# Hybrid FNet and SSD encoder layer: the SSD products of a unit moved to every second slot of the projection

## Chip, cores and metric

The kernel runs on one core of one Trainium2 chip. The metric is the device time of a whole execution in microseconds (us), given as the median of several runs. Five engines work side by side, each through its own queue in order: TensorE (PE, matrix products; its weight loads are listed as PEld), VectorE (DVE), ScalarE (ACT), GpSimd (POOL) and SyncE (SP), which issues nearly all DMA transfers. They wait for one another by semaphores.

## What is computed

Two sequences, of 1024 and 2048 tokens of 1024 features, pass through one encoder layer in float32. Cut to what matters here:

```python
u = rms_norm(h, norm_w)
proj = u @ w_in
z_f, u_f, z_s, xbc, dt_raw = split(proj)
xs, Bm, Cm = split(silu(conv5(xbc)))
# SSD per head, in chunks of 128 tokens, forwards and backwards:
cb     = einsum('bclgn,bcsgn->bclsg', Cc, Bc)
y_diag = einsum('bclsg,bclsgr,bcsgrp->bclgrp', cb, decay, X)
states = einsum('bcsgn,bcsgr,bcsgrp->bcgrpn', Bc, decay_st, X)
y_off  = einsum('bclgn,bcgrpn,bclgr->bclgrp', Cc, prev, exp(a_cs))
y_s = (y_fwd + y_bwd + D * xs) * silu(z_s)     # then a norm by groups
y_f = fnet(u_f) * silu(z_f)
h = h + concat([y_f, y_s]) @ w_out
h = h + (p @ w_ple_in) * sigmoid(h @ w_ple_gate)
out = rms_norm(h, final_norm_w)
```

## The kernel before

**Three stages follow one another.** The first, some 1880 us long, is the projection with the SSD; the second is the Fourier mixing; the third holds the output products. The change touches the first.

The tokens are worked in three blocks of 1024: `P` (the short sequence), `S1` and `S2` (the halves of the long one). A block's projection is cut into **jobs** of 128 output columns, and a job into three **pieces** of 342 tokens. A piece is 24 matmuls into one of three PSUM tiles `ps` (line 361): each float32 product is made of three, high by high, high by low and low by high. The weights of a job come in one DMA (`wr`, line 182); ACT rounds them to the high part `wh` (line 189) and POOL subtracts to get the low part `wl` (line 190).

The 24 heads are worked in twelve **units** of two. A unit's column job `x` is convolved and put through SiLU (DVE and ACT), and its SSD parts then follow, each with a few small float32 matmuls into one of five PSUM banks (the pool `bg`, taken in turn):

- `tokens` (line 421): four transposes into `ptt`; ACT copies them to `xm`.
- `weighted` (line 586): POOL makes `xw` from `xm` and the decay weights. The two buffers of `xw` are shared by the four calls of a unit, `(d, c4)` for direction and half.
- `states` (line 606): products of `xw` and `Bm` into `pst`; DVE runs the state on in `H` (line 617).
- `diag` (line 574): products with the decay tile `R`, into `pd`. `R` is loaded by SP (`rows_in`, three buffers), cut by POOL (line 549), exponentiated by ACT (line 558) and joined by DVE (lines 563 and 565).
- `across` (line 648): products of `H` and `CT` into `po`; DVE adds them to `y` (lines 651 and 652).
- `gated` (line 657): POOL multiplies `y` by the gate. In block `S1` alone it does two more operations, on `er` and `zT` (lines 661 and 662).
- `group_tokens` and `group_cb` do the like once for three units (lines 421 and 525).

**The order is written out by hand.** Time is counted in **slots**, one for each piece. `pre(s, f)` puts a function ahead of the piece of slot s, `post(s, f)` behind it, and `step` runs the functions ahead, the piece, and the functions behind, in the order in which they were registered. Each engine's queue keeps that order. A unit's plan begins at slot s0, and consecutive units of a block are nine slots apart: s0 is 12 + 9u in `P`, 135 + 9u in `S1`, 258 + 9u in `S2`, so even and odd s0 take turns. The weight splits (`wh`, `wl`) were registered first of all; in the steady part they stand ahead of every third slot, at s0, s0 + 3, s0 + 6, s0 + 9 and so on. At a block's end the transposes `pt` of the next block's tokens (line 264) stand behind pieces too and take the same five banks.

So ahead of slot s0 + 9 stands, in POOL's queue: the split of a job's weights, `gated(4)` of the unit before (whose offset is 18 there), then what `weighted` has in this slot.

Of the kernel before, what the change touches and what calls it, by code (L numbers as in the profile page):

```python
# [56 lines left out]
def tile_hybrid_encoder(ctx: ExitStack, tc: tile.TileContext, a):  # L57
# [44 lines left out]
    with ExitStack() as ph:  # L102
# [175 lines left out]
        def pre(s_, fn, *args):  # L278
            assert s_ >= slot[0], (s_, slot[0])
            before.setdefault(s_, []).append((fn, args))  # L280

        def post(s_, fn, *args):
            assert s_ >= slot[0], (s_, slot[0])
            behind_.setdefault(s_, []).append((fn, args))
# [244 lines left out]
        class Unit:  # L529
# [140 lines left out]
            def plan(self, s0):  # L670

                B, g = self.B, self.g
                self.y, self.xw, self.er, self.H, self.R, self.xm = {}, {}, {}, {}, {}, {}
                if self.u % 3 == 0:
                    for k, s_ in enumerate((1, 3) if g else (4, 5)):
                        post(s0 + s_, group_tokens, B, g, 4 * k)
                    for k, s_ in enumerate((6, 7)):
                        post(s0 + s_, group_cb, B, g, 4 * k)
                post(s0 + 7, self.tokens, 0)
                pre(s0 + 8, self.weighted, 0, 0)  # L680
                post(s0 + 8, self.tokens, 4)
                pre(s0 + 6, self.state_in)
                pre(s0 + 9, self.weighted, 1, 4)
                post(s0 + 9, self.states, 0, 0)
                pre(s0 + 10, self.weighted, 0, 4)
                post(s0 + 10, self.states, 1, 4)
                pre(s0 + 11, self.weighted, 1, 0)
                post(s0 + 11, self.states, 0, 4)
                post(s0 + 12, self.states, 1, 0)
                pre(s0 + 11, self.decays, 0)  # L690
                pre(s0 + 13, self.decays, 4)
                for p in range(4):
                    s_ = s0 + 4 + 2 * p
                    pre(s_, self.rows_in, p)
                    pre(s_ + 2, self.rows_cut, p)
                    pre(s_ + 3, self.rows_exp, p)
                    pre(s_ + 4, self.rows_joined, p)
                    post(s_ + 5, self.diag, p)
                post(s0 + 14, self.across, 0)
                pre(s0 + 16, self.gated, 0)  # L700
                pre(s0 + 18, self.out, 0)
                post(s0 + 16, self.across, 4)
                pre(s0 + 18, self.gated, 4)
                pre(s0 + 20, self.out, 4)

        def norm_piece(b, i):

# [44 lines left out]
        for m in range(2, len(coming)):  # L752
            j, k = coming[m], coming[m - 1]
# [19 lines left out]
        with tc.manual_schedule():  # L773
# [30 lines left out]
            for B, js, what in rows_:  # L804
                bi, s0 = B.bi, slot[0]
                if what == "first":
                    q = s0 if bi else s0 + 1
# [459 lines left out]
    fn = q4.tile([P, DM], F32, name="fn")  # L1267
# [116 lines left out]
```

## Time and profile before

| | |
|---|---|
| Median of 3 runs | 2940.09 us (2939.32 to 2940.15) |
| The profiled execution | 2938.98 us, of which the span from first to last instruction is 2937.0 us |
| Mean granted TensorE clock | 0.983 of full speed |
| PE busy | 2806.8 us (96%) |
| DVE, ACT, POOL busy | 2223.1, 1382.3, 1515.5 us (76, 47, 52%) |

In a timeline a row gives the start, the length, the engine, the line, the operation, its output and inputs, the shapes and the number of merged instructions; in brackets stands how long the engine sat idle before it, and what released it. Matmuls overlap, so the distance from one start to the next tells what a matmul costs, not its own length. A float32 product of the SSD shows as two matmul records. In a table of waits a row gives the sum of the waits, their number and the longest. In a table by windows the columns are the length, the busy time of each engine with its number of instructions, the granted PE clock, the share of the DMA engines and GB/s.

### The profile page before, as it was taken

To read this page: it belongs to the slowest core of one execution; us is meant where nothing else is said; L and a number is where in the kernel's file an instruction comes from. 1 tells how busy PE (TensorE), PEld (TensorE's weight loads), DVE (VectorE), ACT (ScalarE), POOL (GpSimd) and SP (SyncE) were. 2 spreads that over 40 slices of the span, in tenths; PEclk is the share of its full clock that TensorE was granted. 3 is DMA by queue.
4 is the path that set the end of the run, shared out by engine and by line. 5 is a ranking of instruction groups with operands and counts; after the bars stand their busy time and mean duration, and the time that the engine had idled before them with its cause. 6 is when DMAs were issued, how large, how long until landed. Compare 5 with 4: busy or idle time off the path is not lost. (4 is left out here: it accounts for less than half of the span.)

```text
span 2937.0 us, 46503 instructions
## 1 busy us (share of the span) xinstructions
PE 2806.8 (96%) x17252; PEld 2551.2 (87%) x17252; DVE 2223.1 (76%) x3412; ACT 1382.3 (47%) x2980; POOL 1515.5 (52%) x1114
## 2 busy tenths in 40 slices
PE   6999999999999999999999999789999899989998
PEld 5999999999999999999999999777777677768887
DVE  3787777687778686778787776797989998766665
ACT  4544465444545564435444444344334533355554
POOL 1255656542667777633656655455877678510000
PEclk9999999999999999999999999889999999999999
DMA  3245565362465665534455454465544654442221
GB/s 99 85 146 153 167 188 168 126 182 83 125 186 165 207 190 157 160 118 116 145 161 157 154 159 132 151 230 213 173 154 145 230 167 140 150 180 80 95 97 62
DMA packets 327998, 440.10 MB, mean 150 GB/s; under 512 B 19824, under 2 KB 250932, under 8 KB 323932
## 3 DMA queue, kind: packets, MB, share of 16 engines
q1 hardware_dynamic: 327484, 436.08, 47.1%
q8 instruction: 136, 2.23, 0.3%
q10 hardware_dynamic: 288, 1.05, 0.1%
q14 instruction: 90, 0.74, 0.1%
HBM read 328.41 MB, written 109.71 MB: 149 GB/s over the span
## 5 line engine op out<-in xcount | busy, mean ns | idle before, releaser
L361 PE MATMUL ps<-uh,wh 128*128 128x342 f32 (+1 forms) x2880 | 955.3, 332 | 12.9 <-ACT uh L267 9.6
L361 PE MATMUL ps<-ul,wh 128*128 128x342 f32 (+1 forms) x2880 | 920.0, 319 | 2.5 <-DVE ul L268 2.5
L361 PE MATMUL ps<-uh,wl 128*128 128x342 f32 (+1 forms) x2880 | 921.7, 320 | 0.4 <-POOL wl L190 0.4
L190 POOL TENSOR_TENSOR wl<-wr,wh 128x1024 fp32r<-128x1024 f32 x120 | 296.3, 2469 | 660.4 <-ACT wh L189 660.4
L361 PEld LDWEIGHTS ps<-uh,wh 128*128 128x128 f32 x2880 | 545.2, 189 | 36.5 <-issue 15.5
L361 PEld LDWEIGHTS ps<-ul,wh 128*128 128x128 f32 x2880 | 548.2, 190 | 4.2 <-DVE ul L268 3.5
L361 PEld LDWEIGHTS ps<-uh,wl 128*128 128x128 f32 x2880 | 544.6, 189 | 1.2 <-POOL wl L190 1.1
L558 ACT ACTIVATE R<-R,lb 128x128 f32<-128x128 f32 x1152 | 352.9, 393 | 16.9 <-POOL R L549 16.8
L549 POOL TENSOR_SCALAR_AFFINE_SELECT R<-R 128x512 f32<-128x512 f32 x288 | 274.3, 974 | 6.8 <-DMA R<-ROWd 6.8
L617 DVE SCALAR_TENSOR_TENSOR H<-H,cd,pst 128x64 f32<-128x64 f32 x888 | 182.7, 276 | 102.7 <-PE pst L606 100.5
L586 POOL TENSOR_TENSOR xw<-xm,wd 128x512 f32<-128x512 f32 x144 | 189.4, 1326 | 137.2 <-ACT xm L423 111.7
L367 ACT COPY raw<-ps 128x342 f32<-128x342 f32 x180 | 78.9, 439 | 339.3 <-PE ps L361 339.2
L1100 PE MATMUL X<-whP,ah 128*128 128x512 f32 x480 | 196.8, 410 | 7.9 <-ACT pu L1109 4.7
L402 DVE SCALAR_TENSOR_TENSOR xT<-raw,cvt,xT 128x1024 f32<-128x1024 f32 x144 | 195.5, 1358 | 2.6
L1100 PE MATMUL X<-whP,al 128*128 128x512 f32 x480 | 193.7, 403 | 1.6 <-DVE al L1071 1.6
L1100 PE MATMUL X<-wlP,ah 128*128 128x512 f32 x480 | 194.2, 405 | 0.1
L1212 POOL TENSOR_TENSOR ht<-ht,pu 128x512 f32<-128x512 f32 x96 | 156.3, 1637 | 63.0 <-ACT pu L1109 44.0
L652 DVE TENSOR_TENSOR y<-y,yt 128x512 f32<-128x512 f32 (+1 forms) x144 | 161.3, 1120 | 5.0
L1071 DVE TENSOR_TENSOR al<-s,ah 128x512 fp32r<-128x512 f32 x144 | 142.9, 1014 | 20.2 <-ACT ah L1070 20.0
L272 ACT ACTIVATE zT<-ps 128x342 f32<-128x342 f32 (+1 forms) x108 | 49.1, 454 | 219.0 <-PE ps L361 218.7
L565 DVE TENSOR_TENSOR R<-R,cb 128x512 f32<-128x512 f32 x144 | 148.4, 1030 | 5.0
L651 DVE TENSOR_TENSOR yt<-po,er 128x512 f32<-128x512 f32 (+1 forms) x144 | 91.2, 634 | 76.0 <-PE po L648 67.8
(264 smaller groups left out, 5812.9 us busy)
## 6 DMA issues: line engine op xcount, KB each, us to landing
R<-ROWd SPq DMA_DIRECT2D x144, 512.0 KB
wr<-in_w_in SPq DMA_DIRECT2D x120, 512.0 KB
er<-EXPd SPq DMA_DIRECT2D x144, 256.0 KB
Hd<-ht SPq DMA_DIRECT2D x48, 512.0 KB
ht<-Hd SPq DMA_DIRECT2D x48, 512.0 KB
y<-Yd SPq DMA_DIRECT2D x46, 512.0 KB
wlP<-WSd SPq DMA_DIRECT2D x21, 1024.0 KB
Yd<-y SPq DMA_DIRECT2D x72, 256.0 KB
```

The source lines that it names most:

```text
L190: G.tensor_tensor(wl, raw, wh.bitcast(F32), op=ALU.subtract)
L361: T.matmul(ps[:, :n], lhsT=wt[:, kt, :], rhs=ut[:, kt, :n], start=(i == 0), stop=(i == 3 * KT - 1))
L402: V.scalar_tensor_tensor(dst, raw[:, k:k + TB], cvt[:, 20 * k + ct:20 * k + ct + 1], dst, op0=ALU.mult, op1=ALU.add)
L549: G.affine_select(out=R, in_=R, pattern=[[0, 2], [0, 2], [sgn, P]], compare_op=ALU.is_ge, fill=NEG, base=0, channel_multiplier=-sgn)
L558: S.activation(R[:, h, d, c, :], R[:, h, d, c, :], AF.Exp, bias=self.B.lb[:, 2 * p + c, hc + h:hc + h + 1])
L565: V.tensor_tensor(E[0], E[0], cb.unsqueeze(1).broadcast_to([P, 2, 2 * P]), op=ALU.mult)
L586: G.tensor_tensor(xw, self.xm[c4].rearrange("p c (h e) -> p c h e", h=2), col(self.B.wd[:, c4:c4 + 4, hc:hc + 2]).broadcast_to([P, 4, 2, 6 ...
L617: V.scalar_tensor_tensor(dst[:, e], H[d][:, cc, e], B.cd[:, cc, hc + h:hc + h + 1], pst[:, c, e], op0=ALU.mult, op1=ALU.add)
L652: V.tensor_tensor(y[:, cr], y[:, cr], t[:, cr], op=ALU.add)
L1071: V.tensor_tensor(al, src, ah.bitcast(F32), op=ALU.subtract)
L1100: T.matmul(ps, lhsT=at[:, k, :], rhs=wt[:, k, :], start=(first and i == 0), stop=(i == 11), skip_group_check=not first)
L1212: return lambda t: G.tensor_tensor(h, h, t, op=ALU.add)
```

## The change

The SSD parts of a unit are put only behind pieces of even slots: a new helper `part` rounds the slot up to the next even one, and `weighted` stands ahead of the slot behind the part that it needs.

```diff
+                def part(o, fn, *args):
+                    o += (s0 + o) % 2
+                    post(s0 + o, fn, *args)
+                    return s0 + o
                 if self.u % 3 == 0:
-                    for k, s_ in enumerate((1, 3) if g else (4, 5)):
-                        post(s0 + s_, group_tokens, B, g, 4 * k)
-                    for k, s_ in enumerate((6, 7)):
-                        post(s0 + s_, group_cb, B, g, 4 * k)
-                post(s0 + 7, self.tokens, 0)
-                pre(s0 + 8, self.weighted, 0, 0)
-                post(s0 + 8, self.tokens, 4)
+                    for k, o in enumerate((1, 3) if g else (4, 5)):
+                        part(o, group_tokens, B, g, 4 * k)
+                    for k, o in enumerate((6, 7)):
+                        part(o, group_cb, B, g, 4 * k)
                 pre(s0 + 6, self.state_in)
-                pre(s0 + 9, self.weighted, 1, 4)
-                post(s0 + 9, self.states, 0, 0)
-                pre(s0 + 10, self.weighted, 0, 4)
-                post(s0 + 10, self.states, 1, 4)
-                pre(s0 + 11, self.weighted, 1, 0)
-                post(s0 + 11, self.states, 0, 4)
-                post(s0 + 12, self.states, 1, 0)
+                pre(part(7, self.tokens, 0) + 1, self.weighted, 0, 0)
+                pre(part(8, self.tokens, 4) + 1, self.weighted, 1, 4)
+                pre(part(9, self.states, 0, 0) + 1, self.weighted, 0, 4)
+                pre(part(10, self.states, 1, 4) + 1, self.weighted, 1, 0)
+                part(11, self.states, 0, 4)
+                part(12, self.states, 1, 0)
...
-                    post(s_ + 5, self.diag, p)
-                post(s0 + 14, self.across, 0)
-                pre(s0 + 16, self.gated, 0)
-                pre(s0 + 18, self.out, 0)
-                post(s0 + 16, self.across, 4)
-                pre(s0 + 18, self.gated, 4)
-                pre(s0 + 20, self.out, 4)
+                    part(9 + 2 * p, self.diag, p)
+                for o, c4 in ((14, 0), (16, 4)):
+                    q = part(o, self.across, c4)
+                    pre(s0 + o + 2, self.gated, c4)
+                    pre(s0 + o + 4, self.out, c4)
```

Where s0 is even, both `tokens` stand at s0 + 8, both `weighted` of the first pair ahead of s0 + 9, the first two `states` with `diag(0)` at s0 + 10, the other two `weighted` ahead of s0 + 11, and the other two `states` at s0 + 12; each `diag` stands one slot later. Where s0 is odd, `tokens(4)` joins `states(0, 0)` at s0 + 9, the middle two `states` stand at s0 + 11, the last at s0 + 13, and `across` at s0 + 15 and s0 + 17. Loads, cuts, exponentials, joins and gates keep their slots. PE's projection is interrupted by SSD groups 346 times before and 190 times now; the matmuls are the same.

On PE, the place is unit 3 of block `S1` (s0 = 162): its second `tokens` (`ptt_9269`), the first two `states` (`pst`) and `diag(0)` (`pd_9340`). The rows `ps` are the first or last matmul of a piece. Before:

```order
L421 MATMUL ptt_9269<-ident_105,xT_8926 128x128 x4
L361 MATMUL ps_9300<-uh0_6616,wh_9102 128x342
...
L606 MATMUL pst_9328<-xw_9226,Bm_8878 128x128 x4
L574 MATMUL pd_9340<-R_9016,xm_9219 64x128 x4
L361 MATMUL ps_9361<-uh1_6774,wh_9102 128x342
...
L606 MATMUL pst_9388<-xw_9284,Bm_8878 128x128 x4
```

The same place of the changed kernel (`ptt_9267` is the second `tokens`, `pst_9368` and `pst_9381` the two `states`):

```order
L421 MATMUL ptt_9267<-ident_105,xT_8904 128x128 x4
L361 MATMUL ps_9300<-uh0_6609,wh_9087 128x342
...
L361 MATMUL ps_9300<-uh0_6609,wl_9088 128x342
L361 MATMUL ps_9340<-uh1_6761,wh_9087 128x342
...
L606 MATMUL pst_9368<-xw_9282,Bm_8937 128x128 x4
L606 MATMUL pst_9381<-xw_9284,Bm_8937 128x128 x4
L574 MATMUL pd_9393<-R_9000,xm_9259 64x128 x4
```

Two pieces now follow each other with nothing between, and both `states` stand behind the second.

In POOL's queue the same unit's `weighted` calls (`xw`), a weight split (`wl`) and the gates of the unit before (`y`, `er`, `zT`) stand in this order before:

```order
L657 TENSOR_TENSOR y_8944<-y_8944,zT_8456 128x512
L661 TENSOR_TENSOR er_8889<-er_8889,elt_154 128x512
L662 TENSOR_TENSOR zT_8456<-er_8889,zT_8456 128x512
L586 TENSOR_TENSOR xw_9226<-xm_9219,wd_7447 128x512
L549 AFFINE_SELECT R_9112<-R_9112 128x2x256 x2
L190 TENSOR_TENSOR wl_9276<-wr_9159,wh_9275 128x1024
L657 TENSOR_TENSOR y_9150<-y_9150,zT_8456 128x512
L661 TENSOR_TENSOR er_9005<-er_9005,elt_154 128x512
L662 TENSOR_TENSOR zT_8456<-er_9005,zT_8456 128x512
L586 TENSOR_TENSOR xw_9284<-xm_9268,wd_7447 128x512
L586 TENSOR_TENSOR xw_9347<-xm_9268,wd_7447 128x512
```

and now:

```order
L549 AFFINE_SELECT R_9097<-R_9097 128x2x256 x2
L190 TENSOR_TENSOR wl_9274<-wr_9159,wh_9273 128x1024
L657 TENSOR_TENSOR y_9135<-y_9135,zT_8437 128x512
L661 TENSOR_TENSOR er_8989<-er_8989,elt_154 128x512
L662 TENSOR_TENSOR zT_8437<-er_8989,zT_8437 128x512
L586 TENSOR_TENSOR xw_9282<-xm_9259,wd_7447 128x512
L586 TENSOR_TENSOR xw_9284<-xm_9266,wd_7447 128x512
L549 AFFINE_SELECT R_9206<-R_9206 128x2x256 x2
L586 TENSOR_TENSOR xw_9400<-xm_9266,wd_7447 128x512
```

The first `xw` of the unit, which stood ahead of the weight split and the gate, now stands behind them.

## The prediction

> **What bounds the kernel now.** First the page's totals, then the table by windows, then PE's waits in the first stage.
>
> ```profile
> span 2937.0 us, 46503 instructions
> PE 2806.8 (96%) x17252; PEld 2551.2 (87%) x17252; DVE 2223.1 (76%) x3412; ACT 1382.3 (47%) x2980; POOL 1515.5 (52%) x1114
> ...
> 300.00:400.00 100.00, 100.00 (x712) 97.27 (x712) 73.97 (x128) 52.80 (x124) 61.66 (x48) 1.00 0.62 189
> 900.00:1000.00 100.00, 99.38 (x704) 95.74 (x703) 78.72 (x135) 50.57 (x117) 66.89 (x53) 1.00 0.60 190
> ...
> PE prw L495 <- ACT acs L473: 4.6, 3, 2.6
> PE pst L606 <- POOL xw L586: 3.4, 9, 0.9
> PE pt L264 <- DVE H L617: 2.6, 2, 2.0
> ```
>
> In the first stage PE is never free: 100.00 us busy of 100, at full clock. The waits come from the window from 100 to 1880 us, and they are the longest three there; PE waits for little more than 10 us in 1780. So what the change is worth is (a) what an interruption of the projection costs on PE itself, and (b) the waits that it removes or makes. POOL and DVE are off the path as long as they hand over in time; (b) asks whether they still do.
>
> **What an interruption costs.** Three places on PE: `diag` alone between pieces, `across` alone (its last four matmuls shown again, from a narrower window), and `diag` with a further group behind it.
>
> ```profile
> 901.76 0.31 PE L361 MATMUL ps<-uh,wl 128*128 128x342 f32 x1
> 902.00 0.66 PE L574 MATMUL pd<-R,xm 128*64 128x128 f32 x8
> 902.59 0.42 PE L361 MATMUL ps<-uh,wh 128*128 128x342 f32 x1
> 902.85 0.31 PE L361 MATMUL ps<-ul,wh 128*128 128x342 f32 x1
> ...
> 906.33 0.32 PE L361 MATMUL ps<-uh,wl 128*128 128x342 f32 x1
> 906.48 1.72 PE L648 MATMUL po<-CT,H 128*128 128x128 f32 x14
> 907.60 0.61 PE L648 MATMUL po<-CT,H 128*128 128x128 f32 x4
> 907.96 0.40 PE L361 MATMUL ps<-uh,wh 128*128 128x342 f32 x1
> 908.20 0.31 PE L361 MATMUL ps<-ul,wh 128*128 128x342 f32 x1
> ...
> 252.77 0.32 PE L361 MATMUL ps<-uh,wh 128*128 128x342 f32 x1
> 252.92 0.32 PE L361 MATMUL ps<-ul,wh 128*128 128x342 f32 x1
> 253.08 0.31 PE L361 MATMUL ps<-uh,wl 128*128 128x342 f32 x1
> 253.32 0.66 PE L574 MATMUL pd<-R,xm 128*64 128x128 f32 x8
> 253.91 1.16 PE L525 MATMUL pc<-CT,BT 128*128 128x128 f32 x8
> 254.82 0.40 PE L361 MATMUL ps<-uh,wh 128*128 128x342 f32 x1
> 255.06 0.32 PE L361 MATMUL ps<-ul,wh 128*128 128x342 f32 x1
> ```
>
> Undisturbed, projection matmuls start 0.157 us apart (252.77 to 253.08 is two steps). The first one behind a group looks dear: the next starts 0.24 us later (907.96 to 908.20), 0.084 more. But it also starts early, close behind the group's last matmul. Whole: from 906.33 to 908.20 are 1.87 us; less two steps of 0.157 the 14 `po` matmuls cost 1.56, 0.111 each, and that is their pace inside the group (906.48 to 907.60 is ten steps, 0.112 each). Going in and out is free. `diag` alone costs 902.85 - 901.76 - 0.31 = 0.78. `diag` with eight `pc` behind it costs 255.06 - 253.08 - 0.31 = 1.67, and apart the two would be 0.78 + 8 x 0.111 = 1.67. **So joining two groups saves nothing:** 156 interruptions fewer are 0 us, and with 0.02 us of reading error each -3 to +3.
>
> **What the change removes.** All nine waits of `pst` for `xw` (3.4 us) are of the old order. In the new one an odd s0 gives POOL longer: below, POOL has its second `xw` 11.7 us after slot s0 + 9 begins, and PE asks for it only after three pieces (3 x 3.77) and that slot's group (4 `ptt`, 8 `pst`, 8 `pd`: 0.44 + 0.89 + 0.67), at 13.3. That is -3.4 us. Even s0 comes next.
>
> **What it adds: POOL in block S1.** The rows are of unit 3, whose slot s0 + 9 begins at 877.52, and of unit 7, which begins at 1059.97.
>
> ```profile
> 877.52 0.40 PE L361 MATMUL ps<-uh,wh 128*128 128x342 f32 x1
> 879.42 2.39 POOL L190 TENSOR_TENSOR wl<-wr,wh 128x1024 fp32r<-128x1024 f32 x1 [2.20 <-ACT wh L189]
> 881.76 1.28 POOL L657 TENSOR_TENSOR y<-y,zT 128x512 f32<-128x512 f32 x1
> 883.00 1.05 POOL L661 TENSOR_TENSOR er<-er,elt 128x512 f32<-128x512 f32 x1
> 884.13 1.65 POOL L662 TENSOR_TENSOR zT<-er,zT 128x512 f32<-128x512 f32 x1
> 885.74 3.48 POOL L586 TENSOR_TENSOR xw<-xm,wd 128x512 f32<-128x512 f32 x2
> 887.29 1.16 PE L606 MATMUL pst<-xw,Bm 128*128 128x128 f32 x8 [0.31 <-POOL xw L586]
> ...
> 1059.97 0.40 PE L361 MATMUL ps<-uh,wh 128*128 128x342 f32 x1
> 1067.84 2.51 POOL L586 TENSOR_TENSOR xw<-xm,wd 128x512 f32<-128x512 f32 x2
> ```
>
> Before, the `xw` ahead of the split was for the first `states`, and these two were for the later ones. Now the chain split, `y`, `er`, `zT` stays, since it hangs on ACT's `wh` and on the slot, and **both** `xw` that PE needs next stand behind it, while PE gets there sooner, for slot s0 + 9 has nothing behind its piece. PE asks after two pieces: 48 x 0.157 + 0.084 = 7.62 us. In unit 3 the first `xw` is ready at 887.29 - 877.52 = 9.77: a wait of 2.1. The eight `pst` then take 0.9, to 10.7, and the second is ready at 885.74 + 3.48 = 889.22, that is 11.7: another 1.0. In unit 7 the pair is shorter: the first, at half of 2.51, ends at 9.13 (1.5 late), the second at 10.38 (0.3 late). Blocked behind the waiting `pst` is all of PE, projection and all, so each microsecond counts in full. Even s0 in S1 means six units; the last has no split in that slot, which leaves five. Ends: 5 x 3.1 = 16, and 5 x 1.3 = 6.5 if POOL also starts 0.2 earlier and only the first wait stays. I take 2.3 each, since a first wait as in unit 3 with a second as in unit 7 is 2.4: **+11.5 us**.
>
> In `P` and `S2` the gate is one operation, and the same place has room:
>
> ```profile
> 400.70 0.40 PE L361 MATMUL ps<-uh,wh 128*128 128x342 f32 x1
> 406.18 2.55 POOL L586 TENSOR_TENSOR xw<-xm,wd 128x512 f32<-128x512 f32 x2
> ```
>
> The pair ends at 408.73, 8.03 us in; the first, near 6.8, is early, and the second is asked for at 7.62 + 0.9 = 8.5. Cost 0, with 0.5 us to spare.
>
> **The clock.** A gap on PE can cost more than itself:
>
> ```profile
> 729.77 0.42 PE L361 MATMUL ps<-uh,wh 128*128 128x342 f32 x1 [2.32 <-DVE zT L273]
> ...
> 729.77:733.60 3.83, 3.83 (x14) 3.83 (x15) 3.03 (x4) 1.27 (x2) 1.57 (x2) 0.56 0.99 303
> 733.60:737.00 3.40, 3.40 (x27) 3.40 (x27) 1.42 (x3) 3.40 (x12) 0.00 (x0) 1.00 0.25 97
> ```
>
> After this gap of 2.32 us the granted clock was 0.56 for 3.83 us, and 14 matmuls took what 24 take: 1.6 us lost. The nine old `xw` waits, 0.9 at most, left no such mark in windows at 1.00. My gaps of 1.5 to 2.1, in unit 3 with another of 1.0 close behind, lie between. I let three of five lose 1.5: **+4.5 us**, ends 0 and 8. The Trainium skill, "TensorE: Matmul & The Clock Gate", part 1, says that the clock falls to half after at least one idle window of about 3.4 us. By that rule none of these gaps would cost more than itself and the sum would be 4.5 lower; the row of 2.32 us speaks against it.
>
> **The rest.** At the two block ends the transposes `pt` wait for banks that DVE's `H` empties (2.6 us before). New there: two `pst` are emptied one behind the other, but PE has `pd` and two `pt` in between; 0, ends -2 and +4. Behind the very last piece one more `states` stands, whose run of `H` is 1.24 us by the row below: +1, ends 0 and 2.
>
> ```profile
> 1868.46 1.24 DVE L617 SCALAR_TENSOR_TENSOR H<-H,cd,pst 128x64 f32<-128x64 f32 x6
> POOL R L549 <- DMA R<-ROWd: 6.8, 3, 3.5
> ```
>
> Where s0 is even, the load of the fourth `R` needs the buffer of the first, whose `diag` is a slot later; SP holds its queue as long. POOL cuts that `R` two slots later and waited for such loads only 6.8 us in the first stage: hidden. DVE gets its evictions in bunches but the same sum; `ps` has three tiles, and the joined `R` of an even s0 now has a slot more. The later stages hold the same instructions, some in another order at the start of the Fourier stage and of the last products: 0, ends -3 and +3.
>
> **Sum**, against the profiled execution (2938.98: span 2937.0 and 1.98 around it; 1.1 below the median 2940.09): 0 - 3.4 + 11.5 + 4.5 + 0 + 1 + 0 = +13.6, so **2952.6 us**. All lower ends give 2934, all upper ends 2971.
>
> **Rivals.**
> 1. *The clock holds* (the rule above): 13.6 - 4.5 = +9.1, 2948.1. For it: no gap before of this very length. Chance 0.20.
> 2. *POOL's chain shortens*, as DVE is quieter beside it and ACT's split comes earlier: 6.5 - 3.4 + 1 = +4.1, 2943.1. For it: unit 7's pair takes 2.51 where unit 3's takes 3.48. Chance 0.20.
> 3. *Faster: an interruption does cost 0.084*, the late second start, and the early first start is no return for it. 156 x 0.084 = 13.1; with rival 2's waits -9.0, 2930.0. It decides if a slot without a group is shorter than 24 x 0.157. Against it: the 1.56 us of 14 `po`. Chance 0.07.
> 4. *DVE's bunches reach PE*: `R` or `H` comes late in every unit. At half a run of `H`, 0.6, that is 36 x 0.6 = 21.6 more, 2974. Against it: DVE's share, 76%. Chance 0.09.
>
> **Chances.** The forecast with its clock losses has 0.42, and 0.02 are left for the unforeseen. Slower by over 0.2% (5.9 us, about what a measurement here can tell from no change) are the forecast, rivals 1 and 4: 0.73 with the rest. Within 0.2%: rival 2, 0.20. Faster: 0.07. The range runs from 2940, below rival 2, to 2966, over the forecast with most of its upper ends; rivals 3 and 4 stay out.
>
> **What would show it.** Right: PE waits for `pst` on `xw` rise from 3.4 to about 11 us, all in S1, two to a unit of odd number, none in `P` and `S2`; the clock falls behind some; two joined pieces and a group still make 48 x 0.157 plus the group. Wrong: no such wait (POOL ahead), a shorter slot (rival 3), or waits on `H` or `R` throughout (rival 4).

## The result and the profile after

| | before | changed |
|---|---|---|
| Median, four runs each | 2939.70 us (2939.22 to 2940.15) | 2965.91 us (2957.86 to 2967.18) |
| Ratio of the runs (that of the medians alone is 1.0089) | | 1.0085, interval 1.0073 to 1.0097 |
| The profiled execution | 2938.98 us (span 2937.0) | 2957.86 us (span 2956.1), the shortest of its four |

The changed kernel is 26.2 us slower in the median and 18.9 us slower in the profiled execution. Two lines of its page, and then PE's waits of the first stage (100 to 1900 us), in the view that the prediction began with:

```profile
span 2956.1 us, 46441 instructions
PE 2816.4 (95%) x17252; PEld 2559.4 (87%) x17252; DVE 2220.9 (75%) x3412; ACT 1384.5 (47%) x2980; POOL 1524.9 (52%) x1114
...
PE pst L606 <- POOL xw L586: 15.4, 9, 4.1
PE prw L495 <- ACT acs L473: 4.7, 3, 2.6
PE ps L361 <- DVE zT L273: 3.3, 1, 3.3
...
PE pt L264 <- DVE H L617: 1.9, 2, 1.0
```

Every engine was busy for the same time within 10 us, with the same number of instructions. The wait of `pst` for `xw` has grown from 3.4 to 15.4 us, and its longest from 0.9 to 4.1. In a narrower window, S1 alone (745 to 1266 us), it is this one row, six waits:

```profile
PE pst L606 <- POOL xw L586: 13.5, 6, 4.1
```

Where the time went shows when the starts of the slots' first matmuls are set side by side, in the two profiled executions (us):

| Stretch | before | changed | difference |
|---|---|---|---|
| start to slot 117 (P) | 609.4 | 613.0 | +3.6 |
| slots 117 to 144 (into S1) | 131.2 | 132.8 | +1.6 |
| slots 144 to 243 (S1, eleven units) | 503.4 | 519.3 | **+15.9** |
| slots 243 to 261 (into S2) | 86.8 | 85.5 | -1.3 |
| slot 261 to the first `pst` behind the last piece (S2) | 540.8 | 542.8 | +2.0 |
| from there to the first matmul of the Fourier stage | 22.0 | 25.9 | **+3.9** |
| the rest | 1043.4 | 1036.8 | -6.6 |

Down to the Fourier stage these are +25.7, which is about the 26.2 of the medians. The last row is the reason why this one execution lost only 18.9; it is taken up in the first experiment.

For S1, each distance from one matmul to the next was held against the median of its kind over both traces (its line, the next one's line, its place in the group). PE's own work is the same: without the single gaps and what half-clock stretches added, the projection from slot 0 to 368 took 1812.7 us before and 1814.2 now. The 15.9 us of S1 are 9.0 more of single gaps (5.5 before, 14.5 now) and 7.8 of longer distances within half-clock stretches (none before), less 0.9 in all other distances. Unit 3 shows both. The timeline of POOL, DVE and PE from its slot s0 + 9, which starts at 887.86:

```profile
889.85 2.41 POOL L190 TENSOR_TENSOR wl<-wr,wh 128x1024 fp32r<-128x1024 f32 x1 [2.09 <-ACT wh L189]
...
892.21 1.84 POOL L657 TENSOR_TENSOR y<-y,zT 128x512 f32<-128x512 f32 x1
892.92 1.67 DVE L565 TENSOR_TENSOR R<-R,cb 128x512 f32<-128x512 f32 x1
...
894.01 1.49 POOL L661 TENSOR_TENSOR er<-er,elt 128x512 f32<-128x512 f32 x1
894.52 4.30 DVE L402 SCALAR_TENSOR_TENSOR CT<-raw,cvt,CT 128x1024 f32<-128x1024 f32 x2
895.58 2.15 POOL L662 TENSOR_TENSOR zT<-er,zT 128x512 f32<-128x512 f32 x1
897.70 3.03 POOL L586 TENSOR_TENSOR xw<-xm,wd 128x512 f32<-128x512 f32 x2
...
899.78 3.48 PE L606 MATMUL pst<-xw,Bm 128*128 128x128 f32 x16 [4.15 <-POOL xw L586]
```

The chain is the forecast one, split, `y`, `er`, `zT`, `xw`, but slower: `y` 1.84 (1.28 before), `er` 1.49 (1.05), `zT` 2.15 (1.65), each beside a DVE instruction. PE gets its first `xw` 11.92 us into the slot, not at 9.77, and stands idle for 4.15. The 16 `pst` matmuls then last 3.48 us, where such a group takes 1.95 at full clock (row of the filled gap, below): the granted clock fell. In the table by windows, the first row is of that place; the others, set on the edges of the clock's stretches, show units 5 and 7:

```profile
899.50:903.30 3.80, 3.52 (x18) 3.41 (x20) 1.38 (x7) 1.95 (x7) 3.45 (x5) 0.56 0.02 4
...
988.10:991.50 3.40, 2.00 (x13) 1.72 (x11) 1.80 (x2) 0.44 (x1) 3.32 (x3) 1.00 0.73 206
991.50:994.90 3.40, 2.77 (x25) 2.44 (x26) 1.54 (x8) 0.00 (x0) 3.40 (x5) 1.00 0.07 21
...
1083.70:1087.10 3.40, 1.36 (x10) 1.08 (x10) 3.37 (x3) 2.28 (x4) 3.40 (x4) 1.00 0.00 0
1087.10:1090.50 3.40, 3.40 (x18) 2.84 (x19) 3.33 (x7) 1.66 (x6) 3.40 (x3) 0.50 0.02 5
```

In both units PE is idle for about 2.04 us in all. In unit 5 an edge cuts this into 1.40 and 0.63, and the clock stays at 1.00; in unit 7 all of it falls into one stretch, and the next is granted 0.50.

### The profile page after: what moved, and what is told of

Same layout as the page of the kernel before. It is cut to its first block, busy times and chain, and to the rows that moved or that the text cites. A ratio compares the mean times of both kernels' runs of the same rounds, so it can differ in the third digit from the quotient of the medians.

```text
span 2956.1 us, 46441 instructions
## 1 busy us (share of the span) xinstructions
PE 2816.4 (95%) x17252; PEld 2559.4 (87%) x17252; DVE 2220.9 (75%) x3412; ACT 1384.5 (47%) x2980; POOL 1524.9 (52%) x1114
## 3 DMA queue, kind: packets, MB, share of 16 engines
q10 hardware_dynamic: 288, 1.05, 0.1%
## 5 line engine op out<-in xcount | busy, mean ns | idle before, releaser
L361 PE MATMUL ps<-uh,wh 128*128 128x342 f32 (+1 forms) x2880 | 943.0, 327 | 12.6 <-ACT uh L267 8.4
L549 POOL TENSOR_SCALAR_AFFINE_SELECT R<-R 128x512 f32<-128x512 f32 x288 | 285.7, 1014 | 8.8 <-DMA R<-ROWd 7.6
L402 DVE SCALAR_TENSOR_TENSOR xT<-raw,cvt,xT 128x1024 f32<-128x1024 f32 x144 | 222.5, 1545 | 2.6
L586 POOL TENSOR_TENSOR xw<-xm,wd 128x512 f32<-128x512 f32 x144 | 175.6, 1233 | 77.4 <-ACT xm L423 67.8
L563 DVE TENSOR_TENSOR R<-R 128x512 f32<-128x512 f32 x144 | 136.7, 949 | 72.4 <-issue 70.0
L565 DVE TENSOR_TENSOR R<-R,cb 128x512 f32<-128x512 f32 x144 | 155.4, 1079 | 6.3 <-ACT cb L526 1.0
L657 POOL TENSOR_TENSOR y<-y,zT 128x512 f32<-128x512 f32 x72 | 109.6, 1523 | 97.7 <-DVE y L652 97.7
L606 PE MATMUL pst<-xw,Bm 128*128 128x128 f32 x1056 | 140.8, 283 | 15.4 <-POOL xw L586 15.4
```

The costliest lines, as they stand in the source:

```text
L361: T.matmul(ps[:, :n], lhsT=wt[:, kt, :], rhs=ut[:, kt, :n], start=(i == 0), stop=(i == 3 * KT - 1))
L402: V.scalar_tensor_tensor(dst, raw[:, k:k + TB], cvt[:, 20 * k + ct:20 * k + ct + 1], dst, op0=ALU.mult, op1=ALU.add)
L549: G.affine_select(out=R, in_=R, pattern=[[0, 2], [0, 2], [sgn, P]], compare_op=ALU.is_ge, fill=NEG, base=0, channel_multiplier=-sgn)
L565: V.tensor_tensor(E[0], E[0], cb.unsqueeze(1).broadcast_to([P, 2, 2 * P]), op=ALU.mult)
L586: G.tensor_tensor(xw, self.xm[c4].rearrange("p c (h e) -> p c h e", h=2), col(self.B.wd[:, c4:c4 + 4, hc:hc + 2]).broadcast_to([P, 4, 2, 6 ...
L606: T.matmul(pst[:, c, :], lhsT=B.Bm[self.g][:, c4 + c, :], rhs=xw[:, c, :, :].rearrange("p h e -> p (h e)"), start=True, stop=True)
```

## The experiments

All are timed against the kernel before on the same chip. "S1" is slots 144 to 243 of the profiled execution, "tail" the time from the start of the last piece's last matmul to the first `pm` of the Fourier stage (22.1 before). "Gaps" and "clock" are the two parts taken apart above (5.5 and 0 before). The ratio is taken over all runs of both kernels and is not the quotient of the medians. All lengths are those of the one profiled execution of each run.

| Run | Median (range) us | Ratio to before, interval | S1: length, gaps, clock | Tail |
|---|---|---|---|---|
| changed, again | 2965.88 (2960.5 to 2966.4) | 1.0092, 1.0076 to 1.0108 | 519.6, 14.5, 7.9 | 25.9 |
| late gate | 2943.78 (2938.2 to 2953.2) | 1.0024, 1.0011 to 1.0037 | 502.6, 5.6, 0 | 26.4 |
| new in P, S2 | 2946.26 (2940.0 to 2951.9) | 1.0027, 1.0017 to 1.0037 | 503.4, 5.5, 0 | 26.9 |
| new in S1 | 2965.47 (2962.9 to 2968.6) | 1.0094, 1.0078 to 1.0109 | 522.2, 14.5, 10.6 | 22.6 |
| gap filled | 2959.98 (2954.9 to 2960.5) | 1.0068, 1.0056 to 1.0081 | 514.7, 6.5, 1.7 | 26.2 |
| `xw` ahead | 2948.36 (2938.5 to 2951.9) | 1.0024, 1.0014 to 1.0035 | 504.1, 5.5, 1.5 | 26.6 |
| before, `xw` ahead | 2932.48 (2922.6 to 2937.1) | **0.9975**, 0.9965 to 0.9985 | 497.6, 0.7, 0 | 21.9 |
| new in P | 2938.82 (2931.3 to 2943.6) | 0.9995, 0.9986 to 1.0005 | 503.5, 5.5, 0 | 22.1 |
| new in S2 | 2946.41 (2943.6 to 2950.8) | 1.0030, 1.0018 to 1.0042 | 503.5, 5.5, 0 | 26.8 |
| S2, `across` first | 2942.36 (2939.6 to 2945.3) | 1.0014, 1.0005 to 1.0023 | 503.4, 5.5, 0 | 24.1 |
| new in S2, again | 2945.39 (2940.6 to 2949.0) | 1.0026, 1.0016 to 1.0036 | 503.4, 5.5, 0 | 27.0 |

**The changed kernel again**, no edit.

> The changed kernel once more, unaltered, for its spread: four executions gave 2957.86, 2965.10, 2966.72 and 2967.18, where four of the kernel before lie within 0.93 us. Theory (late xw, and the clock behind the gap): the same spread again, 2957 to 2968, and the profile taken here shows the nine or so waits for xw in S1 in the same units, while the number of half-clock stretches in S1 differs from the 20.5 us of the first profile. Rival (the 8 us come from the later stages, or from one unit whose wait varies): the half-clock time in S1 is the same and the difference stands elsewhere.

The waits came in the same units, and S1 with its half-clock time was the same (17.1 us in both, not 20.5 as written there). So the rival is right about these two profiled executions: this one gained 2.9 us on the first profile up to the last piece, and lost 5.6 behind the last piece. The slower executions, at 2965 to 2967, have no profile. Of this program's two profiles, the first and then this one, at the same place of the Fourier stage:

```profile
1994.59 6.77 POOL L1042 TENSOR_TENSOR yv<-yv,Z 128x1024 f32<-128x1024 f32 x2 [4.57 <-DMA Z<-ZFd]
1994.88 0.68 DVE L986 TENSOR_TENSOR fold<-Ue 128x512 f32<-128x512 f32 x1
...
1991.74 5.20 POOL L1042 TENSOR_TENSOR yv<-yv,Z 128x1024 f32<-128x1024 f32 x2 [5.19 <-DMA Z<-ZFd]
1992.50 2.22 DVE L859 TENSOR_TENSOR wlP<-wlP,whP 128x512 fp32r<-128x512 f32 x1
1994.64 2.85 DVE L986 TENSOR_TENSOR fold<-Ue 128x512 f32<-128x512 f32 x1
...
2000.42 0.79 PE L1024 MATMUL pr<-th,ql 128*128 128x512 f32 x1 [4.05 <-DVE fold L990]
```

Once POOL's two multiplications took 6.77 us and DVE's `fold` 0.68; the other time POOL took 5.20 and DVE's two instructions 2.22 and 2.85, and PE came to wait 4.05 us and lost the clock. That stretch, from half to three quarters of the stage's `pr` matmuls, took 24.2 us in the one profile and 32.0 in the other. Of all thirteen profiles only the late gate's has the short form as well (24.2). In these two POOL's first multiplication there took 4.4 us; in the other eleven it took 2.4 to 2.8, and the stretch 30.2 to 33.0 (31.8 in the kernel before). So some 8 us in the last row of the stretches are chance, and not the change's.

**Late gate.** The changed kernel with the gate of S1 a slot later:

```diff
-                    pre(s0 + o + 2, self.gated, c4)
+                    pre(s0 + o + 2 + (c4 == 4 and B.b["n"] == "S1"), self.gated, c4)
```

> The changed kernel, but in block S1 the second gate of a unit (y, er, zT on POOL) stands one slot later, so that the next unit's two xw stand ahead of it in POOL's queue. Theory (late xw): split ends about 4.3 us into slot s0 + 9, both xw by 7.0, PE asks at 7.6: the S1 gaps (14.5 us in the first profile) and the half-clock loss behind them (7.8) go, so 2935 to 2940, and the executions agree within 2 us. Rival (joined parts bunch work on DVE and ACT, and PE pays for that throughout): 2950 or more. Rival (the wait only moves to the gate's readers): no pst wait, but a new wait of the same size on y or zT.

S1 fell from 519.3 to 502.6 us, and no half-clock stretch was left there. The median is 22 us lower, but 4 above the range expected. PE's waits in S1 (745 to 1250 us):

```profile
PE ptt L421 <- DVE xT L411: 3.9, 2, 2.9
PE ptt L421 <- DVE raw L332: 0.8, 1, 0.8
PE pst L606 <- POOL xw L586: 0.3, 1, 0.3
```

Part of what is left is thus a new wait, of `ptt` for DVE. It is neither for `y` nor for `zT`, as the second rival had it; that DVE comes late is the first rival's mechanism, in small. The executions also spread over 15 us, against the expectation.

**The new plan in P and S2 alone, and in S1 alone**; both plans stand in the kernel, and the block picks one:

```diff
+            def plan(self, s0):
+                (self.plan_new if self.B.b["n"] != "S1" else self.plan_old)(s0)
```

> The new plan in blocks P and S2 alone, the old one in S1: 103 of the 156 interruptions fewer stay. Theory (all the loss is POOL's chain in S1, an interruption costs nothing): 2936 to 2944, no spread. Rival (an interruption costs 0.084 us): 8.7 us faster than before, 2931. Rival (bunching costs in every unit): two thirds of the loss, 2952 to 2958.

> The new plan in block S1 alone, the old one in P and S2. Theory (all the loss is POOL's chain in S1): 2954 to 2966, nearly all the loss, with the spread of the changed kernel. Rival (bunching in every unit): a third of the loss, 2946 to 2950, little spread.

With the old plan in S1, its length is as before, and two thirds of the joins bring nothing. But 7.6 us of loss are left, 2 over the range expected, and the runs spread over 12 us: the loss is not all S1's. With the new plan in S1 alone, S1 is 18.8 us longer, with the gaps of the changed kernel (14.5) and more clock losses (10.6, in another phase of the stretches), and nearly the whole loss is there. Some 8 us of it are not S1's: the automatic scheduler gave this kernel's later stages another order, and from the last piece on they took 1076.6 us in its profile (of its slowest execution), against 1065.5 before. What in that order costs them was not taken apart.

**Gap filled.** Matmuls into the same bank, overwritten at once, ahead of the first `states` in S1's units 1, 3, 5, 7, 9:

```diff
+                if b["n"] == "S1" and u in (1, 3, 5, 7, 9) and (d, c4) == (0, 0):
+                    for c in 2 * [c for c in order]:
+                        T.matmul(pst[:, c, :], lhsT=B.Bm[self.g][:, c4 + c, :],
+                                 rhs=B.Bm[self.g][:, c4 + c, :], start=True, stop=True)
```

> The changed kernel with eight float32 matmuls more (1.78 us, their product is overwritten by the next) ahead of the first states in units 1, 3, 5, 7 and 9 of S1: 40 matmuls more, inside the gaps in which PE waits for xw. The idle stretches of 2.9, 4.1, 1.9, 1.6 and 2.2 us shrink to about 1.1, 2.3, 0.1, 0 and 0.4. Theory (PE idle for some 1.8 us within one 3.41 us stretch of a fixed grid halves the clock of the next stretch): all half-clock stretches in S1 go but perhaps one behind unit 3, the work added is hidden in the waits, so S1 is 5 to 7 us shorter than the changed kernel's 519.5 and the median 2956 to 2961 (changed kernel 2966). Rival (the clock does not follow the gaps; what is lost is the wait alone): S1 519 or longer, 2964 to 2970.

The timeline at unit 3 (matmul, POOL's two `xw`, matmul), and the wait over S1:

```profile
891.95 1.95 PE L607 MATMUL pst<-Bm 128*128 128x128 f32 x16
...
894.19 3.03 POOL L586 TENSOR_TENSOR xw<-xm,wd 128x512 f32<-128x512 f32 x2
...
896.26 3.66 PE L610 MATMUL pst<-xw,Bm 128*128 128x128 f32 x16 [2.37 <-POOL xw L586]
...
PE pst L610 <- POOL xw L586: 5.5, 6, 2.4
```

With 8.9 us of work more on PE, S1 is 4.6 us shorter than in the changed kernel (5 to 7 were expected) and the median 5.9 lower. One half-clock stretch is left, behind unit 3, whose remaining gap is 2.37. The theory holds: the clock follows the gaps, and its losses are a cost beside the waits.

**`xw` ahead**, in the changed kernel and in the kernel before: in S1 the last gate of a unit is registered by the next unit, behind the first pair of `weighted`. The edit in the kernel before:

```diff
-                pre(s0 + 18, self.gated, 4)
+                if B.b["n"] == "S1" and self.u < NU - 1:
+                    B.late = s0 + 18, self.gated, 4
+                else:
+                    pre(s0 + 18, self.gated, 4)
...
                 pre(s0 + 9, self.weighted, 1, 4)
+                if B.b["n"] == "S1" and self.u:
+                    pre(*B.late)
```

> The changed kernel, in S1 with both xw of a unit's first pair ahead of the last gate of the unit before, in the same slot; the gate is 2.5 us later only, not a slot as in the run with the late gate. Theory (late xw): no pst wait for xw and no half-clock stretch in S1 behind it; the wait for xT that the late gate brought (3.9 us) stays away too, S1 500 us or less against 503.4 before, and the median 2938 to 2943: P and S2 keep their 3 to 4 us over the kernel before. Rival (any delay of the gate is paid on another wait): S1 503 or more with a wait on xT or zT, 2943 to 2948.

> The kernel before with the same edit alone: in S1 weighted(1, 4) stands ahead of the gate of the unit before, nothing else moves. Theory: the nine waits of 0.37 to 0.9 for xw (3.4 us) go, S1 500 against 503.4 and 3 us less in all, 2933 to 2938. Rival (the chain behind it, gate and xT, becomes late): as before or slower, 2938 to 2942.

In the changed kernel the first row below is what is left in S1, and in the kernel before the second row is all:

```profile
PE ptt L421 <- DVE xT L411: 3.9, 2, 2.9
...
PE pd L574 <- ACT R L558: 0.7, 1, 0.7
```

The changed kernel's `xw` waits go (0.2 us left), but the waits for `xT` stay, as the rival had it, and the median, 2948.36, is just above even the rival's range. But this run turned out to repeat the late gate: POOL ran its 260 instructions of S1 in the same order in both, the gates within 0.1 us of each other up to the one half-clock stretch here, and the ratios are the same, 1.0024. So it doesn't tell whether the waits for `xT` come with the new plan or with the later gate; the kernel before with its gate one `xw` later has none. In the kernel before, the nine waits go and nothing takes their place: S1 497.6, **2932.48 us, the best time of all**, a quarter of a per cent under the kernel before.

**P alone and S2 alone**, picked as above.

> The new plan in block P alone. The instructions of the Fourier stage and of the products then stand on PE and SP in the order that they have in the changed kernel (but for 5 rows), while S1 and S2 are as before. Theory (the other order of the later stages costs some 4 us in the median, as the runs with that order stand 1.4 to 5.4 us beyond what their first stage explains): first stage 3 to 4 us later as in the run with P and S2, less 1.5 for S2, and 4 behind it, 2944 to 2948. Rival (the later stages only vary by the phase of the clock's grid): the first stage's 2 to 3 us alone, 2940 to 2943.

> The new plan in block S2 alone; the later stages then have the order of the run with the kernel before and xw ahead (47 rows of PE differ from the kernel before). Theory (the other order of the changed kernel costs 4 us): here only S2's own 1.5 to 2.5 us, two waits of 0.8 and less of the block's end, 2939 to 2943. Rival (any change of the order costs): 2944 or more.

P alone is no slower than before, with the changed kernel's order of the later stages. So that order costs nothing, and my theory of it falls. S2 alone costs 7.5 us. Its profile has 2.2 us more between slot 261 and the last piece and a tail longer by 4.7. In the tail no pieces are left, and PE shows the SSD groups alone (the last piece's `pst`, the fourth `pd`, `po`, the Fourier stage's `pm`), before, then in S2 alone:

```profile
1871.68 0.83 PE L606 MATMUL pst<-xw,Bm 128*128 128x128 f32 x6
...
1877.31 3.54 PE L648 MATMUL po<-CT,H 128*128 128x128 f32 x16 [0.38 <-DVE H L617]
...
1893.65 1.19 PE L970 MATMUL pm<-wbd,bd 128*128 128x128 f32 x4 [10.45 <-DVE Ue L980]
...
1872.60 1.72 PE L606 MATMUL pst<-xw,Bm 128*128 128x128 f32 x14
...
1878.66 0.66 PE L574 MATMUL pd<-R,xm 128*64 128x128 f32 x8 [2.60 <-DVE H L617]
1881.37 1.12 PE L574 MATMUL pd<-R,xm 128*64 128x128 f32 x8 [2.05 <-issue]
1882.42 5.61 PE L648 MATMUL po<-CT,H 128*128 128x128 f32 x30
...
1899.29 1.20 PE L1009 MATMUL pm<-wbd,bd 128*128 128x128 f32 x4 [11.27 <-DVE Ue L1022]
```

The first `po` begins 5.6 us after the start of the `pst` behind the last piece before, and 9.8 now. The last unit's s0 is odd (357); `part` puts the fourth `diag` and `across(0)` behind the same slot, `diag` first, and that waits for the `R` joined last.

**`across` first.** The new plan in S2, and in its last unit `across(0)` ahead of the fourth `diag`:

```diff
+                    if p < 3 or self.u < NU - 1:
                         part(9 + 2 * p, self.diag, p)
...
                     q = part(o, self.across, c4)
+                    if c4 == 0 and self.u == NU - 1:
+                        part(15, self.diag, 3)
```

> The new plan in S2 alone, and in its last unit the fourth diag stands behind across(0) instead of ahead of it. Theory (the tail is 4 us longer because across(0) waits behind the fourth diag, whose R is joined last, with no piece left to hide it): the Fourier stage's first matmul stands 22 to 23 us after the last piece's last matmul instead of 25.9 to 26.9, and the median is 3 to 4 us under that of the new plan in S2 (2946.4), 2942 to 2944. Rival (the Fourier stage starts by the loads, not by the tail): 26 us again, 2945 to 2948.

> The new plan in S2 alone once more, beside the run with across(0) first. Both theories: 2944 to 2949, the Fourier stage's first matmul at 26 to 27 us.

```profile
1873.72 1.72 PE L606 MATMUL pst<-xw,Bm 128*128 128x128 f32 x14
...
1880.82 3.35 PE L648 MATMUL po<-CT,H 128*128 128x128 f32 x16 [0.29 <-DVE H L617]
...
1897.63 1.19 PE L1012 MATMUL pm<-wbd,bd 128*128 128x128 f32 x4 [11.11 <-DVE Ue L1022]
```

The tail fell from 26.8 and 27.0 to 24.1 us (22 to 23 were expected), and the median by 3.0, to within the expectation. 2.0 us over the kernel before remain in the tail: two `states` (x14) now stand behind the last piece ahead of the `pd` where one stood (x6), and DVE has one more run of `H` to do before `across`.

## Why the prediction was right or wrong

The forecast was 2952.6 us, +13.6 to the profiled execution; measured were 2965.91 in the median and +18.9 in the profiled execution. The median lies inside the range by 0.1 us, and that is luck: the mechanism was right, but several terms were too small, all in the same direction. By its steps:

- **Joining two groups saves nothing: right.** PE's own work is equal within 1.5 us with 156 interruptions fewer, where rival 3 had 13.1 less, and new plans in P or S2 bring no gain. Rival 3 falls.
- **The nine old `xw` waits go (-3.4): right.** All waits of S1 are now in the units named, and odd s0 has none.
- **New `xw` waits in S1 (+11.5): place and mechanism right, size too small.** They are 13.5 us. Two to a unit was wrong: they are six in five units, and in unit 3 one wait of 4.15 stands for the 2.1 and 1.0. The step read the durations of POOL's chain from the old order, where DVE did other work beside it. The new order gives DVE its join and the convolution just then, and the first `xw` came 2.15 us later than forecast. That DVE's work is what slowed POOL is read from the timeline; no run tested it by itself. Rival 2 (the chain shortens) went the wrong way.
- **The clock (+4.5): mechanism right, size too small.** 7.8 us in S1 in this execution and 10.6 in the run with S1 alone; the filled gap shows that it is the gaps' doing. Rival 1 falls; its ground, that no gap before was of this length, overlooked the two rows below, from the end of S1 in the kernel before: PE idle for 2.00 us, and then a mean clock of 0.61. By the rule of the Trainium skill, "TensorE: Matmul & The Clock Gate", part 1, that it takes an idle window, only unit 3 could have lost clock; four units did.

```profile
1256.30:1258.30 2.00, 0.00 (x0) 0.00 (x0) 1.97 (x9) 0.67 (x2) 0.00 (x0) 1.00 1.07 255
1258.30:1262.70 4.40, 4.36 (x20) 4.39 (x21) 3.25 (x5) 3.74 (x10) 2.17 (x1) 0.61 0.47 154
```

- **P and S2 at 0, with 0.5 us to spare: wrong.** S2 is 2 us longer, in every profile with the new plan there. P is 2.4 us longer in the mean of seven profiles (609.4 to 613.0 up to slot 117) against six with the old plan (608.0 to 610.3), though the runs with the new plan in P alone show no loss in the median. The waits of `pst` for `xw` in these blocks are 1.9 us (15.4 less 13.5), and one of `ptt` 0.8; the rest was not found. In a unit of S2 the cause looks like that of S1, `y` at 1.84 us beside DVE's join:

```profile
1657.42 1.84 POOL L657 TENSOR_TENSOR y<-y,zT 128x512 f32<-128x512 f32 x1
...
1662.77 1.16 PE L606 MATMUL pst<-xw,Bm 128*128 128x128 f32 x8 [0.83 <-POOL xw L586]
```

- **Block ends at 0: right** in the sum (+1.6 and -1.3), in part by luck: the first holds one half-clock stretch more than before, the second one fewer.
- **The tail (+1): wrong, +3.9.** The step counted one more run of `H`. It missed that rounding to an even slot put `diag(3)` ahead of `across(0)`, where no piece hides the wait for `R`; the last experiment gave 2.8 of 4.8 us back.
- **The later stages at 0: right**, apart from chance. The long and the short form of the Fourier stage differ by some 8 us whatever the change, and of the two executions compared the changed kernel's had the short one. Without that, +18.9 would be about +26, the median's loss.
- **Rival 4 (DVE's bunches reach PE)** is there in small: `ptt` waits for `xT` 3.9 us in S1 once the `xw` waits are gone. What makes DVE late there was not tested.

So the mis-sized terms are S1's waits (+2), its clock (+3 to +6), P and S2 (+5) and the tail (+3): 13 to 16 us, about the 13 between forecast and median.

## What to carry to other kernels

When work moves on an engine's queue, read its duration from a place where the neighbour engine does what it will do then, and not from the old place: in unit 3 the gate's three operations on POOL were 30 to 44% slower in their new company, though over all of S1 their means moved by only -5 to +13%. Where rounding or joining puts two groups behind one slot, look at the places without cover, the last unit above all, and at the order inside the group. And before thinning out interruptions, measure one: here they were free, while the order of one `xw` and a gate on an engine far from its limit (POOL, 52%) was worth 7 us without any of it.

## What the runs showed of the hardware

- **The clock is decided in stretches of 3.41 us on a grid that is fixed within an execution**: all half-clock stretches of a profile start on one grid, whose phase to the first instruction differs (3.16 us before, 1.69 and 1.81 in two profiles of the changed kernel). In the first stages of thirteen profiles (from 110 us on, outside half clock), PE was idle for 1.80 us or more of a stretch 34 times, and 33 times the next ran at half clock (the exception had 1.84); of twelve stretches with 1.2 to 1.77 us none did so. So half a stretch is enough, a gap of 2 us counts or not by where the grid cuts it, and one half-clock stretch cost 1.56 us (7.8 in five).
- **POOL and DVE hold each other up.** In the Fourier stage the same two DVE instructions took 0.68 us, or 2.22 and 2.85 while POOL multiplied; then POOL was the quicker one (5.20 against 6.77). The Trainium skill, "SBUF — State Buffer", section "SBUF: two separate sides", says that the two share a port pair, an exclusive lock that whoever starts first holds for its whole instruction; of DVE's instructions it names those in a two-port mode or with two inputs from SBUF, as `wlP` and `fold` have here. Both traces agree with it, and which of the two came first went with 6 to 9 us of that stretch in all thirteen profiles.
